# A 1 KB read of b ahead of the first loads, in a two-layer matmul kernel on one core

## The chip, the cores and the metric

The kernel runs on one core of a Trainium2 chip. The metric is the device time in microseconds (us) of one execution. The time before is 117.33 us, the median of 3 runs (117.23 to 117.46).

The engines are named as in the profile: PE is TensorE (PEld its weight loads), DVE is VectorE, ACT is ScalarE, POOL is GpSimd, SP is SyncE, which here does nothing but issue transfers.

## What is computed

```python
h = np.matmul(a, b)            # a: 1024 x 1024, b: 1024 x 2048, float32
h = 0.5 * h * (1 + np.tanh(np.sqrt(2 / np.pi) * (h + 0.044715 * h ** 3)))
return np.matmul(h, c).astype(np.float32)      # c: 2048 x 1024
```

## The kernel before

**Tiling.** M = K = P = 1024 and N = 2048, in tiles of 128 rows. The first product is made transposed: its result, after the gelu, is `hT`, with N on the partitions, in two halves of 512 columns of M. TensorE therefore needs a transposed (`aT`, by transposes through TensorE, line 145, copied out of PSUM by VectorE, line 146) and b as it lies in memory (`b1`, `b2`). The first 512 columns of N are computed plainly (`mm1`, line 114). The rest of the first product, and the whole second product, use a scheme with seven block products in place of eight (class `Seven`, products on line 212), with sums and differences of blocks on VectorE (line 170).

**Order.** The schedule is written out by hand: each engine does its instructions in the order of the program. Waits between engines are on semaphores that the framework sets. Transfers issued by SyncE and ScalarE share eight completion counters, given out in turn in the order of the program; GpSimd's transfers have eight others.

**Loads.** SyncE issues five loads at the start (lines 75 to 79), in float32, in this order:

- line 75: the first quarter of a for M's first half (`sta[:, 0, 0]`, 512 KB, 1 KB pieces),
- line 76: b's rows 0 to 255, first 512 columns (`stb[:, 0:2]`, 512 KB, 2 KB pieces; for each partition the rows p and p + 128),
- line 77: the same quarter of a's columns for M's second half (512 KB),
- line 78: the second quarter for the first half (512 KB),
- line 79: b's rows 256 to 383 (256 KB).

VectorE and ScalarE cast what these bring to bf16 (lines 110 and 108). GpSimd waits for the first of them by a copy of one column (`gate`, line 81), and then issues everything else as loads that cast on the way: the rest of a (`abq`, line 86), the rest of b (lines 89, 92, 98, 101) and all of c (line 104). Until the first data come, TensorE multiplies zeros (`stir`, line 125).

The order of the work at the start, on TensorE: five `stir`s; the transposes of the first quarter; matmuls for k = 0 and part of k = 1, once b's first rows are cast; the transposes of line 77's quarter (the group of eight at 8.47 us); and so on through the quarters, the last of which is `abq`'s fourth for M's second half.

**Stores.** The results leave in `done2` (line 431), called for each 128 x 512 block of the output, each by one transfer from SyncE (line 429), except that the second block to leave, `(i, l, j) == (0, 0, 1)`, is stored as two transfers of 256 columns. Three more stores of part of a block come at the very end (line 376), one of them from ScalarE. The transfers issued by SyncE and ScalarE are 24 in all: 5 loads, 16 in `done2`, 3 at the end.

A tile of 128 x 16 float32 called `room` is set aside among the constants and not used (line 55).

Of the kernel before, what the change touches and what calls it, by code (L numbers as in the profile page):

```python
# [9 lines left out]
F32 = mybir.dt.float32  # L10
# [9 lines left out]
def kernel(ctx, tc, a, b, c, out):  # L20
    nc = tc.nc
# [3 lines left out]
    H = 512  # L25
# [8 lines left out]
    consts = ctx.enter_context(tc.tile_pool(name="consts", bufs=1))  # L34
# [11 lines left out]
    def pieces(tag, bufs, shape, dt, name):  # L46
        return small.tile(shape, dt, name=name, tag=tag, bufs=bufs)
# [4 lines left out]
    gate = consts.tile([128, 1], F32, name="gate")  # L52
    g = consts.tile([128, 1], F32, name="g")

    consts.tile([128, 16], F32, name="room")

    c_sb = keep.tile([128, NT, P], BF16, name="c_sb")
    hT = [keep.tile([128, NT, H], BF16, name=f"hT{h}") for h in range(2)]
# [10 lines left out]
    def a_part(h, q):  # L69
        return av[:, 4 * h:4 * h + 4, ds(q * 256, 256)]  # L70

    def b_part(q):
        return bv[:, 2 * q:2 * q + 2, 0:H]

    nc.sync.dma_start(out=sta[:, 0, 0], in_=a_part(0, 0))
    nc.sync.dma_start(out=stb[:, 0:2], in_=b_part(0))
    nc.sync.dma_start(out=sta[:, 1, 0], in_=a_part(1, 0))
# [21 lines left out]
    for n in range(2):  # L99
        for k in range(0, KT, 4):  # L100
            nc.gpsimd.dma_start(out=b2[:, k:k + 4, ts(n, H)],
                                in_=bv[:, k:k + 4, ds(1024 + n * H, H)])
# [325 lines left out]
    def store(mt, q0, w, ot, eng=None):  # L428
        (eng or nc.sync).dma_start(out=out[ts(mt, 128), ds(q0, w)], in_=ot)

    def done2(i, l, j, p):
        if (i, l) == (1, 0):
            ot = pieces("o", 4, [128, H], F32, "ot")
            nc.vector.tensor_copy(ot, p)
            p = ot
        n = 2 if (i, l, j) == (0, 0, 1) else 1
        for q in range(n):
            r = ds(q * (H // n), H // n)
            store(4 * i + j, l * H + q * (H // n), H // n, p[:, r])

    def between2(n):
        if n == "P1":
# [11 lines left out]
        elif n == "P73":  # L454
            two.t4(two.t[1], 4)

    seven(two, done2, between2)


# [28 lines left out]
```

## Time and profile before

| What | Value |
|---|---|
| Median of 3 runs | 117.33 us (117.23 to 117.46) |
| The profiled execution, its own time | 117.6 us |
| Its span, from the first to the last instruction | 115.8 us |
| Granted TensorE clock | 1.00 |
| PE busy | 110.7 us (96%) |
| PEld busy | 77.1 us (67%) |
| DVE busy | 90.1 us (78%) |
| ACT busy | 51.4 us (44%) |
| POOL busy | 17.3 us (15%) |
| Chain that ended last | PE 79%, DMA 13%, POOL 5% |
| SyncE's queue (q1) | 4592 packets, 6.42 MB |
| GpSimd's queue (q0) | 8672 packets, 9.31 MB |

All times within the execution are counted from the start of the span. In a row of the timeline, the first number is the start, the second the time from the first start to the last end of the merged instructions, then the engine, the line, the operation, what it writes and reads, and how many there are; in brackets, the idle time of that engine just before, and what ended it. In the chain of waits, each row is a stretch of time that lay on the path to the last instruction: start, length, and what it was spent on. In the table by stretches, a row has the stretch, its length, each engine's busy time, then the granted clock, the DMA engines' share and the GB/s moved.

### The profile page before, as it was taken

The page shows a single profiled execution, that of the slowest core. Times are in us where ns is not written, and L with a number is a line of the kernel's source. Part 1 is how long each engine was busy: PE and PEld are TensorE (multiplying, and loading weights), DVE is VectorE, ACT ScalarE, POOL GpSimd, SP SyncE. Part 2 cuts the span into 40 slices and gives each one's busy share as a digit, 9 for nine tenths or more (in the row PEclk, how much of TensorE's full clock was granted, in tenths as well). Part 3 has the DMA queues.
Part 4 walks back from the last instruction along what each step waited for, and adds up shares of the span by engine and source line. Part 5 has one row for each costly group of instructions (what it writes and reads, how often), then busy time and mean ns, then how long its engine had stood idle before and what let it go on. Part 6 is the DMA issues. An engine that isn't in the chain of part 4 may idle for free.

```text
span 115.8 us, 1473 instructions
## 1 busy us (share of the span) xinstructions
PE 110.7 (96%) x544; PEld 77.1 (67%) x550; DVE 90.1 (78%) x108; ACT 51.4 (44%) x86; POOL 17.3 (15%) x29
## 2 busy tenths in 40 slices
PE   7889999999999999999999999999999999999990
PEld 6545555445777447888886444588888888888870
DVE  0247747689999998944789999999999986964581
ACT  5053000799268998066699339700043992000000
POOL 2497754222332000000000000000000000000000
PEclk9999999999999999999999999999999999999999
DMA  3999999999999999998000000070000002004994
GB/s 74 296 381 221 200 199 204 204 207 207 205 210 210 211 212 212 212 210 163 9 0 0 6 0 0 0 272 0 0 0 0 0 0 94 2 27 173 364 358 166
DMA packets 13414, 15.94 MB, mean 138 GB/s; under 512 B 736, under 2 KB 9184, under 8 KB 13408
## 3 DMA queue, kind: packets, MB, share of 16 engines
q0 software_dynamic: 8672, 9.31, 47.6%
q1 hardware_dynamic: 4592, 6.42, 15.7%
q10 hardware_dynamic: 144, 0.13, 0.3%
q8 instruction: 4, 0.07, 0.2%
q14 instruction: 2, 0.02, 0.0%
HBM read 20.97 MB, written 4.19 MB: 217 GB/s over the span
## 4 chain that ended last, share of the span: by engine, by line
PE 79%; DMA 13%; POOL 5%; issue 0%; DVE 0%
PE ps L212 76%; DMA abq<-in_a_dram 10%; DMA sta<-in_a_dram 3%; POOL abq L86 3%; PE ps L114 2%; POOL b L89 1%; POOL gate L81 1%; PE pt L145 1%; POOL b L92 0%; DVE ot L375 0%
## 5 line engine op out<-in xcount | busy, mean ns | idle before, releaser
L212 PE MATMUL ps<-x,s 128*128 128x512 f32 x128 | 29.6, 391 | 0.0
L212 PEld LDWEIGHTS ps<-x,s 128*128 128x128 f32 x128 | 24.0, 188 | 5.1
L212 PE MATMUL ps<-x,x 128*128 128x512 f32 x96 | 22.9, 394 | 0.0
L212 PEld LDWEIGHTS ps<-x,x 128*128 128x128 f32 x96 | 18.0, 188 | 3.9
L114 PE MATMUL ps<-aT,b 128*128 128x512 bf16 x62 | 15.7, 379 | 0.3 <-DVE b L110 0.2
L298 ACT ACTIVATE v<-ps 128x512 f32<-128x512 f32 x10 | 6.0, 598 | 19.1 <-PE ps L212 19.1
L212 PE MATMUL ps<-c_sb,hT 128*128 128x512 bf16 (+2 forms) x78 | 14.1, 336 | 0.1
L212 PE MATMUL ps<-x 128*128 128x512 f32 x56 | 13.2, 393 | 0.0
L212 PEld LDWEIGHTS ps<-x 128*128 128x128 f32 x56 | 10.2, 188 | 2.7 <-ACT u L298 0.4
L212 PEld LDWEIGHTS <-hT 128*128 128x128 bf16 x80 | 7.1, 98 | 7.0 <-issue 0.5
L118 ACT ACTIVATE hT<-ps 128x512 bf16<-128x512 f32 x14 | 7.3, 596 | 9.6 <-PE ps L114 9.6
L118 ACT ACTIVATE hT<-ot 128x512 bf16<-128x512 f32 x18 | 10.4, 623 | 2.1 <-DVE ot L303 2.0
L146 DVE COPY aT<-pt 128x512 bf16<-128x512 bf16 x16 | 6.7, 422 | 5.5 <-PE pt L145 5.4
L212 PE MATMUL ps<-aT,b 128*128 128x512 bf16 x46 | 10.6, 379 | 0.1
L303 DVE TENSOR_TENSOR ot<-ps,u 128x512 f32<-128x512 f32 x10 | 6.7, 688 | 5.2 <-ACT u L298 5.2
L303 DVE TENSOR_TENSOR ot<-ps,v 128x512 f32<-128x512 f32 x10 | 6.7, 688 | 4.9 <-DMA out_dram<-ot 3.9
L170 DVE TENSOR_TENSOR x<-c_sb 128x1024 fp32r<-128x1024 bf16 x8 | 9.2, 1216 | 0.0
L114 PEld LDWEIGHTS <-b 128*128 128x128 bf16 x64 | 5.7, 97 | 4.5 <-DVE b L110 0.3
L212 PEld LDWEIGHTS <-b 128*128 128x128 bf16 x48 | 4.6, 97 | 5.7 <-issue 0.3
L104 POOL DMA_DIRECT2D c_sb<-in_c_dram x8 | 5.6, 703 | 13.4 <-DMA b<-in_b_dram 11.1
L170 DVE TENSOR_TENSOR x<-b 128x1024 fp32r<-128x1024 bf16 (+1 forms) x4 | 7.0, 1751 | 0.6 <-issue 0.6
L298 ACT ACTIVATE u<-ps 128x512 f32<-128x512 f32 x10 | 5.9, 597 | 3.4 <-PE ps L212 3.2
(44 smaller groups left out, 110.7 us busy)
## 6 DMA issues: line engine op xcount, KB each, us to landing
c_sb<-in_c_dram POOLq DMA_DIRECT2D x8, 512.0 KB, 19.7
out_dram<-ot SPq DMA_DIRECT2D x14, 256.0 KB, 2.1
b<-in_b_dram POOLq DMA_DIRECT2D x6, 512.0 KB, 15.6
sta<-in_a_dram SPq DMA_DIRECT2D x3, 512.0 KB, 6.2
abq<-in_a_dram POOLq DMA_DIRECT2D x5, 256.0 KB, 8.0
stb<-in_b_dram SPq DMA_DIRECT2D x1, 512.0 KB, 5.4
b<-in_b_dram POOLq DMA_DIRECT2D x2, 256.0 KB, 8.3
stb<-in_b_dram SPq DMA_DIRECT2D x1, 256.0 KB, 7.2
```

The lines of the kernel that those rows point to most:

```text
L81: nc.gpsimd.tensor_copy(gate, sta[:, 0, 0, 3, 0:1])
L86: nc.gpsimd.dma_start(out=abq[:, q, h], in_=a_part(h, q))
L89: nc.gpsimd.dma_start(out=b1[:, 2 * q:2 * q + 2, 0:H], in_=b_part(q))
L104: nc.gpsimd.dma_start(out=c_sb[:, t:t + 2], in_=cv[:, t:t + 2])
L114: nc.tensor.matmul(p, b1[:, k, ts(t, 128)], aT[:, h, k], start=(k == 0), stop=(k == KT - 1))
L118: nc.scalar.activation(hT[h][:, t], p, AF.Gelu_apprx_tanh)
L145: nc.tensor.transpose(pt[:, n, ts(m, 128)], ab[:, m, ts(n, 128)], ident)
L146: nc.vector.tensor_copy(aT[:, h, 2 * q + n], pt[:, n])
L170: nc.vector.tensor_tensor(out=dst[:, r], in0=x[:, r], in1=y[:, r], op=op)
L212: nc.tensor.matmul(p[:, ds(c0, w)], l[:, k, ts(j, 128)], r[:, k, ds(c0, w)], start=(start and k == 0), stop=(k == self.kt - 1), skip_group ...
L298: nc.scalar.activation(st, p, AF.Copy)
L303: nc.vector.tensor_tensor(out=ot, in0=p, in1=st, op=ADD)
```

## The change

One transfer is put ahead of SyncE's five loads. It reads 16 float32 (64 bytes) from each of b's rows 0, 16, 32, ..., 240 into the first 16 partitions of `room`, which nothing reads. And the block that was stored by two transfers is stored by one, so that SyncE's and ScalarE's transfers are 24 as before.

```diff
-    consts.tile([128, 16], F32, name="room")
+    room = consts.tile([128, 16], F32, name="room")
...
+    nc.sync.dma_start(out=room[0:16], in_=b.rearrange("(x y) n -> x y n", y=16)[0:16, 0, 0:16])
     nc.sync.dma_start(out=sta[:, 0, 0], in_=a_part(0, 0))
     nc.sync.dma_start(out=stb[:, 0:2], in_=b_part(0))
     nc.sync.dma_start(out=sta[:, 1, 0], in_=a_part(1, 0))
...
             nc.vector.tensor_copy(ot, p)
             p = ot
-        n = 2 if (i, l, j) == (0, 0, 1) else 1
-        for q in range(n):
-            r = ds(q * (H // n), H // n)
-            store(4 * i + j, l * H + q * (H // n), H // n, p[:, r])
+        store(4 * i + j, l * H, H, p)
```

## Prediction

> **What bounds the kernel now.** I read the chain of waits first, then the timeline of the first 25 us, then the stretches' table of the loads. The chain says where an edit can count at all:
>
> ```profile
> 0.74 3.70 DMA sta<-in_a_dram
> 4.49 0.70 POOL gate L81
> ...
> 10.15 11.43 DMA abq<-in_a_dram
> 21.58 0.05 issue
> 21.63 0.40 PE pt L145 x4
> ...
> 27.73 11.44 PE ps L212 x49
> ...
> 39.21 23.73 PE ps L212 x105
> ...
> 73.79 39.11 PE ps L212 x188
> ...
> 112.93 0.29 DVE ot L375
> ```
>
> From 21.63 on it is TensorE alone to the end: 91 us in which it hardly waits. So a microsecond won or lost in TensorE's start is won or lost at the end, and nothing between 22 us and the last stores is worth anything unless TensorE is made to wait. Before 21.6 it is loads. The timeline shows which landing TensorE's early work hangs on:
>
> ```profile
> 4.46 0.69 DVE L110 CAST ab<-sta 128x1024 bf16<-128x1024 f32 x1 [4.46 <-DMA sta<-in_a_dram]
> 6.62 0.36 DVE L110 CAST b<-stb 128x128 bf16<-128x128 f32 x2 [0.55 <-DMA stb<-in_b_dram]
> 6.90 1.47 PE L114 MATMUL ps<-aT,b 128*128 128x512 bf16 x6 [0.17 <-DVE b L110]
> 7.99 0.43 DVE L110 CAST ab<-sta 128x512 bf16<-128x512 f32 x1 [0.68 <-DMA sta<-in_a_dram]
> 8.47 0.62 PE L145 MATMUL pt<-ident,ab 128*128 128x128 bf16 x8
> 21.62 0.23 PEld L145 LDWEIGHTS <-abq 128*128 128x128 bf16 x4 [0.64 <-DMA abq<-in_a_dram]
> ```
>
> Each of SyncE's loads is used at once when it lands: 4.44 (first quarter of a), 6.59 (b's first 256 rows), 7.97 (the next quarter of a). From 8.47 TensorE runs with gaps of a tenth at most, except one of about 0.3 us ahead of 21.63, where the last cast load of a lands. That load cannot come sooner than the stream ahead of it. So the whole front hangs on the stream of loads, and it moves as one: SyncE's 2.36 MB first, GpSimd's cast loads behind them.
>
> **How fast that stream runs.** SyncE has issued everything by 3.53 us, long before the data are in:
>
> ```profile
> 0.74 0.42 SPq L75 DMA_DIRECT2D sta<-in_a_dram  x1
> 1.22 0.50 SPq L76 DMA_DIRECT2D stb<-in_b_dram  x1
> 1.77 0.46 SPq L77 DMA_DIRECT2D sta<-in_a_dram  x1
> 2.27 0.51 SPq L78 DMA_DIRECT2D sta<-in_a_dram  x1
> ```
>
> ```profile
> 1.80:2.50 0.70, 0.70 (x3) 0.61 (x2) 0.00 (x0) 0.43 (x2) 0.00 (x0) 1.00 0.75 110
> 2.50:4.00 1.50, 1.50 (x5) 1.15 (x5) 0.00 (x0) 0.00 (x0) 0.00 (x0) 1.00 1.07 350
> 4.00:5.50 1.50, 1.07 (x9) 0.65 (x7) 0.69 (x1) 0.00 (x0) 1.01 (x2) 1.00 0.93 253
> 5.50:8.50 3.00, 2.49 (x17) 1.29 (x16) 1.55 (x5) 1.45 (x3) 3.00 (x5) 1.00 1.07 373
> ```
>
> The last number of a row is GB/s. There are two slow places. One is the start, 110 GB/s: the first packets of a. The other is 4.0 to 5.5 us, 253 GB/s, which is when b's first 256 rows are read. The landings say the same: the 512 KB of b take 6.59 - 4.44 = 2.15 us, the two loads of 512 KB of a behind them 7.97 - 6.59 = 1.38 and 9.37 - 7.97 = 1.40. So 2.15 - 1.38 = **0.77 us** are lost on b's first rows. Rows 256 to 383 of b, loaded last, do not show it: 256 KB from 9.37 to 10.07, 0.70 us, half of 1.40. The packet records agree: a 2 KB packet takes 84 ns, but between 4.0 and 6.1 us some sixty of b's 256 take 130 to 500 ns; among the last 128 none does.
>
> **The change, part by part.**
>
> 1. *One more issue at the head of SyncE's queue.* SyncE's five loads follow each other at 0.48, 0.55, 0.50 and 0.55 us; the smallest transfers on this queue (the last stores, 64 KB in 128 rows) still take 0.33 to 0.39 us to issue, and some 0.05 lies between. For sixteen rows I take the low end, 0.33 + 0.05 = **0.38 us**. The trace has no issue of sixteen rows, so the bounds are 0 (all of the issue time goes with the number of rows) and 0.55 (a full load's step); 0.38 is the nearest row. All five loads move back by it, and nothing hides it: the first quarter of a is waited for by VectorE and GpSimd from 0 to 4.46 us.
>
> 2. *1 KB more to move.* Sixteen packets against 2,000 on this queue: nothing by size. If each of sixteen engines takes one, its wait lies in the 0.38 us in which the next load is not there yet.
>
> 3. *b's first rows are touched before they are needed.* The touched rows, 0, 16, ..., 240, span just the 2 MB that the 512 KB load reads. What it saves isn't shown by any row: between 0 and the whole 0.77. Less than nothing has a ground too small to price, 1 KB being added. I take the whole 0.77: b's rows 256 to 383 have the same pitch and packet size and no loss, so the loss goes with being first in b, and a's slow 0.7 us at the start is of the same kind; both are over once a tensor has been read from. That is nearer to "first use" than to "how it is laid out".
>
> 4. *The start of a.* At 110 instead of 350 GB/s, 0.70 us lose 0.70 x (350 - 110)/350 = 0.48 us. If that slowness belongs to the first use of the queue rather than of a, the touch takes it upon itself: between 0 and 0.48 saved. I take 0: the touch reads b, not a.
>
> 5. *The store that is not split* (at 75.1 and 75.5 us, SyncE). One issue of 0.46 us goes, in a stretch where SyncE next waits for VectorE (the store at 76.06) and then has nothing until 95 us. The chain there is TensorE. Nothing, and from the third block on the stores stand in the same places of the same eight completion counters, since one more load and one store less cancel.
>
> 6. *No new wait.* Nobody reads the touched tile. What waits behind the new issue are SyncE's five loads (counted in 1) and, through line 81's copy, GpSimd's cast loads: their issue from 5.14 on moves by up to 0.38. Their first packets appear at 8.8 us, as SyncE's run dry, so I count the drain as their limit, not the issue.
>
> **Sum.** The first quarter of a lands at 4.44 + 0.38 = 4.82; b at 6.59 + 0.38 - 0.77 = 6.20; the next quarter of a at 7.97 - 0.39 = 7.58. VectorE, in order: cast to 5.53, copy of the first transposes 6.03 to 6.45, then b's cast at 6.45 instead of 6.62. So the first matmuls win only 0.17, but they have 0.27 to spare ahead of 8.47, and the transposes there start near 8.1. From there on all landings and TensorE stand **0.39 us earlier**, the last cast load included. The profiled execution took 117.6 us (span 115.8, and 1.8 around it), so it would be 117.2; the median of the runs is 117.33, from which I take the same 0.39: **116.94**.
>
> A rule of the Trainium skill speaks against item 3. "DMA: Bandwidth & Descriptors", section "Latency and other measured facts", reports copies at half rate when rows lie a large power of two apart, whatever was read before, and infers that they meet in one memory channel. The load of b's first rows alternates between rows 1 MB apart, and the last 256 KB of b do not, so the slow stretch would be the pattern's by that rule. The touch would save nothing and the sum would be +0.38. Against it stands a: its quarters alternate between rows 512 KB apart, at 373 GB/s.
>
> **Rivals.**
>
> - *Nothing is bought* (0.26): b's slowness is its access pattern's, or something else at 4 to 6 us, or the touch reaches too few engines. Then only item 1 is left: 117.33 + 0.38 to 0.55 = 117.71 to 117.88. Slow packets go on until 6.1, well past the first packet of each engine, which speaks for it.
> - *Half is bought* (0.18): a first use costs a, by item 4, 0.48; if b's costs as much and the rest is pattern, the saving is eaten by the issue: 117.33 + 0.38 - 0.48 = 117.23, within 0.2%.
> - *The start is spared too* (0.06): 0.39 + 0.48 earlier, 116.46.
> - *The cast loads become late* (0.08, slower): GpSimd's issue hangs on the first quarter of a, which lands 0.38 later. If their descriptors are what 8.8 us waits for, and not the drain, their stream moves to 9.2, a hole opens behind SyncE's, and the landing at 21.58, for which TensorE waits already, comes 0.38 later: 117.71. It decides as soon as the first cast packets come later than SyncE's last. Against it: 3.7 us between issue and first packet, and no pause of the engines at 8.8.
>
> My forecast, 0.39 earlier (0.42), has its own range of 116.7 to 117.1, by the issue's size.
>
> **How the numbers follow.** About 0.2%, 0.23 us, is what a measurement here can tell from no change. Faster: 0.42 + 0.06 = 0.48. Same: 0.18. Slower: 0.26 + 0.08 = 0.34. The range runs from 116.5 (the start spared) to 117.85 (a full issue, nothing bought).
>
> **What would show it.** Item 1: the first sta issue at about 1.1, VectorE's first cast at about 4.85. Item 3: from that landing to b's cast 1.4 to 1.6 us and not 2.15, and a rate near 350 GB/s in that stretch. The sum: transposes of the third group near 8.1 instead of 8.47, the last cast load at about 21.2. Wrong: a first cast at 4.85 with b's landing at 7.0; a first cast at 4.46 (the issue costs nothing, or the start is spared); cast packets that begin after 9 us with engines idle before; any new wait after 25 us.

## The result and the profile after

The changed kernel took 117.70 us, the kernel before 117.27 us (medians of 14 runs each), and the ratio of the times is **1.0041** (95% interval 1.0027 to 1.0055): 0.48 us slower by the ratio, 0.43 by the medians. One of the changed kernel's 14 runs, 119.32 us at a granted clock of 0.983, is left out of the ratio. I had forecast 0.39 us faster. The time lies inside the range that I gave, on the wrong side, next to that of the rival "nothing is bought" (117.71 to 117.88).

Line numbers of the changed kernel are one higher from line 76 on. Its timeline at the start (start, length, engine, line, operation, tiles; in brackets the idle time before and what ended it):

```profile
0.74 0.39 SPq L75 DMA_DIRECT2D room<-in_b_dram  x1
1.19 0.41 SPq L76 DMA_DIRECT2D sta<-in_a_dram  x1
...
5.14 0.69 DVE L111 CAST ab<-sta 128x1024 bf16<-128x1024 f32 x1 [5.14 <-DMA sta<-in_a_dram]
...
7.02 0.36 DVE L111 CAST b<-stb 128x128 bf16<-128x128 f32 x2 [0.26 <-DMA stb<-in_b_dram]
...
8.38 0.55 DVE L111 CAST ab<-sta 128x512 bf16<-128x512 f32 x1 [0.66 <-DMA sta<-in_a_dram]
...
8.99 0.62 PE L146 MATMUL pt<-ident,ab 128*128 128x128 bf16 x8 [0.17 <-DVE ab L111]
```

The touch takes 0.39 us to issue and 0.06 to hand over, so every load behind it is issued **0.45 us** later (1.19 against 0.74). The casts that wait for the loads move by 0.68, 0.40 and 0.39 us: VectorE's first cast from 4.46 to 5.14, b's cast from 6.62 to 7.02, that of line 77's quarter (line 78 here) from 7.99 to 8.38. One profile's landings scatter by some 0.35 us (see the first experiment), so these agree with 0.45. Nothing clear of that scatter is won back: the trace tells a load's landing in sixteen steps, and by the middle one b's first rows come 2.06 us behind the first quarter of a, against 2.03 before. The table by stretches, each moved by 0.45 us against the one of before, so that the same loads stand in the same rows (last number GB/s):

```profile
2.25:2.95 0.70, 0.70 (x3) 0.61 (x2) 0.00 (x0) 0.00 (x0) 0.00 (x0) 1.00 0.70 120
2.95:4.45 1.50, 1.50 (x5) 1.15 (x5) 0.00 (x0) 0.00 (x0) 0.00 (x0) 1.00 1.07 332
4.45:5.95 1.50, 0.99 (x4) 0.28 (x3) 0.69 (x1) 0.00 (x0) 0.78 (x2) 1.00 0.88 276
5.95:8.95 3.00, 2.63 (x18) 1.50 (x18) 1.67 (x5) 1.51 (x3) 3.00 (x5) 1.00 1.04 365
```

110, 350, 253, 373 before; 120, 332, 276, 365 now. Both slow places are still there: the start, and the stretch in which b's first 256 rows are read, although sixteen of those rows had been touched and had landed by 2.2 us. The chain of waits of the changed kernel:

```profile
2.19 6.17 DMA sta<-in_a_dram
8.36 0.02 issue
8.38 0.56 DVE ab L111
8.94 0.05 issue
8.99 0.62 PE pt L146 x8
...
25.18 87.99 PE ps L213 x408
```

It now leads from line 78's load (line 77's in the kernel before) by one cast to TensorE, which does not wait again. The wait of 0.3 us ahead of 21.63 is gone: in the kernel before's profiled execution the last cast load of a landed late, at 21.58, here at 20.49. It was one straggler: fifteen of that load's sixteen steps had come by 19.92. That is why the spans differ by only 0.2 us (115.8 and 116.0) where the third group of transposes differs by 0.52 (8.47 and 8.99). These are one execution each; the medians differ by 0.43.

### The profile page after: what moved, and what is told of

It is laid out like the page before. It is cut to its first block, busy times and chain, and to the rows that moved or that the text cites. A ratio compares the mean times of both kernels' runs of the same rounds, so it can differ in the third digit from the quotient of the medians.

```text
span 116.0 us, 1479 instructions
## 1 busy us (share of the span) xinstructions
PE 111.5 (96%) x550; PEld 77.4 (67%) x550; DVE 90.0 (78%) x108; ACT 51.4 (44%) x86; POOL 17.3 (15%) x29
## 3 DMA queue, kind: packets, MB, share of 16 engines
q1 hardware_dynamic: 4480, 6.43, 15.5%
## 4 chain that ended last, share of the span: by engine, by line
PE 90%; DMA 5%; SPq 1%; DVE 1%; issue 0%
PE ps L213 76%; PE ps L115 11%; DMA sta<-in_a_dram 5%; PE pt L146 3%; DVE ab L111 0%; SPq L77 0%; SPq L76 0%; SPq L75 0%; DVE ot L376 0%
## 5 line engine op out<-in xcount | busy, mean ns | idle before, releaser
L115 PE MATMUL ps<-aT,b 128*128 128x512 bf16 x64 | 16.1, 379 | 0.0
L213 PE MATMUL ps<-aT,b 128*128 128x512 bf16 x48 | 10.7, 379 | 0.0
```

Of the source, the lines that this page charges most:

```text
L115: nc.tensor.matmul(p, b1[:, k, ts(t, 128)], aT[:, h, k], start=(k == 0), stop=(k == KT - 1))
L213: nc.tensor.matmul(p[:, ds(c0, w)], l[:, k, ts(j, 128)], r[:, k, ds(c0, w)], start=(start and k == 0), stop=(k == self.kt - 1), skip_group ...
```

## The experiments

"Before" in the ratios is the kernel before, run on the same chip in the same session. Its own time was 117.20 to 117.26 us. Theory N, formed from the profile after: the touch buys nothing and costs its issue at the head of SyncE's queue.

**The store alone** (e1_store_one): the kernel before with

```diff
-        n = 2 if (i, l, j) == (0, 0, 1) else 1
-        for q in range(n):
...
+        store(4 * i + j, l * H, H, p)
```

> The kernel before with only the store edit: the second block leaves in one transfer, 23 transfers in all. Theory N (the whole loss is the extra issue at the head of SyncE's queue): ratio to before 1.000, within 0.15%, every landing before 22 us where it was. Rival S (the loss is, at least in part, the store's): ratio 1.001 to 1.004.

Ratio 0.9996 (0.9974 to 1.0017). The store is worth nothing that could be measured, as item 5 had it. The landings did not stay where they were: in this profile the first cast came at 4.12 instead of 4.46 and line 77's quarter was cast at 8.34 instead of 7.99, though the loads are those of the kernel before. So a landing read from one profile is good to some 0.35 us; the issue times, and the ratios over several runs, are firmer.

**The touch from another queue** (e2_touch_on_act):

```diff
-    nc.sync.dma_start(out=room[0:16], in_=b.rearrange("(x y) n -> x y n", y=16)[0:16, 0, 0:16])
+    nc.scalar.dma_start(out=room[0:16], in_=b.rearrange("(x y) n -> x y n", y=16)[0:16, 0, 0:16])
```

> The changed kernel with the same 1 KB read issued by ScalarE at 0.74 us, so that SyncE's loads keep their place. Theory N (the touch buys nothing, only its issue costs): ratio to before 1.000, first cast at 4.46, b's cast at 6.6, transposes of the third group at 8.45. Theory F (the touch spares b a first use, and the issue ate it): b's cast 0.2 to 0.7 us sooner, at 5.9 to 6.4, ratio 0.994 to 0.998. Rival X (the sixteen small packets themselves disturb the loads): first cast later than 4.6, ratio above 1.001.

Ratio 1.0009 (0.9987 to 1.0032). The timeline:

```profile
0.74 0.45 ACTq L75 DMA_DIRECT2D room<-in_b_dram  x1
...
6.59 0.36 DVE L111 CAST b<-stb 128x128 bf16<-128x128 f32 x2
...
7.94 0.54 DVE L111 CAST ab<-sta 128x512 bf16<-128x512 f32 x1 [0.52 <-DMA sta<-in_a_dram]
```

b's cast at 6.59 (6.62 before) and line 77's quarter at 7.94 (7.99): the touch saves nothing, even when it delays nothing. Only the first cast is later, 4.70; one engine's share of that load landed late, the middle one of its sixteen steps at 4.07 as before (4.13).

**The touch behind the loads** (e8_touch_last): the same line, moved below line 79's load.

> The changed kernel with the same 1 KB read issued behind SyncE's five loads instead of ahead of them. Theory N (the price is the place at the head of the queue): ratio to before 1.000, within 0.15%, loads issued and landing as in the kernel before. Rival (the read itself disturbs the stream, or the transfers' counters do): ratio 1.002 or more.

Ratio 1.0007 (0.9987 to 1.0028); b's cast at 6.56, line 77's quarter at 7.95. With the same packets and the same 24 transfers, the loss of 0.41% is gone: the price is the place at the head of the queue.

**Two touches** (e14_two_touches): the touch's line twice, the second into `room[32:48]`.

> The changed kernel with the 1 KB read issued twice at the head of SyncE's queue. Theory N (the loss is the issues'): SyncE's first large load issued at 1.64, first cast at 5.1 to 5.6, ratio to before 1.007 to 1.009, twice the loss. Rival (the loss is a single event of the first transfer): ratio 1.003 to 1.005, as with one.

SyncE's first large load was issued at 1.64 and cast at 5.16; b's cast came at 7.53, line 77's quarter at 8.91, each about 0.5 us later than with one touch, so the issue adds up as theory N has it. But the ratio is 1.0155 (1.0100 to 1.0210), about twice what I expected. The table by stretches shows the rest (the number before the last two is the granted clock):

```profile
5.04:8.46 3.42, 1.88 (x15) 1.23 (x15) 2.02 (x5) 0.93 (x2) 3.27 (x5) 1.00 0.98 312
8.46:11.87 3.41, 3.41 (x16) 1.76 (x14) 1.67 (x4) 1.76 (x5) 3.21 (x5) 0.50 1.25 291
```

In the first of these stretches TensorE, waiting for the later loads, was busy 1.88 of 3.42 us; in the next it was granted half its clock. But this is the profile of a run of 120.20 us, one of two in six with a granted clock of 0.98; the other four, at 0.995 to 1.000, still took 118.52 to 119.43. So the clock explains a part of the excess, and the rest is open. More on the clock below.

**The touch of a** (e3_touch_a): the same, with a's rows 0, 32, ..., 480.

```diff
-    nc.sync.dma_start(out=room[0:16], in_=b.rearrange("(x y) n -> x y n", y=16)[0:16, 0, 0:16])
+    nc.sync.dma_start(out=room[0:16], in_=a.rearrange("(x y) n -> x y n", y=32)[0:16, 0, 0:16])
```

> The changed kernel with the 1 KB read from a's rows 0, 32, ..., 480 in place of b's. If the slow start of the first load is the first use of a, it goes: the first cast comes at about 4.6 to 4.75 instead of 5.14, and the ratio to before is 1.000 or below. If the start is slow whatever was touched (theory N), it is as in the changed kernel: first cast at 4.9 to 5.15, ratio 1.003 to 1.005.

Ratio 1.0038 (1.0010 to 1.0066), first cast at 4.81, b's cast at 7.08, line 77's quarter at 8.44. The first cast lies between the two expectations and is 0.33 sooner than with b touched; the later landings, which set the time, are as with b touched. The same issue, the same loss.

What, then, makes b's first load slow? Four runs moved it about.

**b's load in two** (e4_split_b):

```diff
-    nc.sync.dma_start(out=stb[:, 0:2], in_=b_part(0))
+    nc.sync.dma_start(out=stb[:, 0], in_=bv[:, 0, 0:H])
+    nc.sync.dma_start(out=stb[:, 1], in_=bv[:, 1, 0:H])
```

(and the store not split).

> The kernel before with line 76 split in two loads, b's rows 0 to 127 and then 128 to 255, so that no load alternates between rows 1 MB apart; one store is not split, so 24 transfers. Theory P (b's slow stretch is the alternation's): 253 GB/s in 4.0 to 5.5 us becomes 340 or more, the next quarter of a (line 77's) is cast at 7.2 to 7.5 us instead of 7.99, ratio 0.994 to 0.997. Theory F (first use of b): the first of the two is the slow one and the quarter of a stays near 7.99, ratio about 1.000, k = 0 starting earlier.

Ratio 1.0077 (1.0045 to 1.0110); 200 GB/s in 4.0 to 5.5 us. The first 256 KB landed 1.69 us after the quarter of a (4.74 to 6.43), the second 0.66 us later, at full speed; line 77's quarter was cast at 8.54. The time is longer than by either expectation. So it is not the alternation between rows 1 MB apart.

**a before b** (e5_a_second): lines 76 and 77 exchanged.

> The kernel before with lines 76 and 77 in the other order: both halves of a's first quarter, then b's first rows. Theory T (whatever is read at 4 to 6 us is slow, b or not): 4.0 to 5.5 us stays under 300 GB/s with a in it, and b behind it comes at full speed, 1.4 us after the quarter of a. Theory F (b's first large read is slow wherever it stands): a at 340 GB/s or more up to 5.8 us, then b takes 1.8 to 2.2 us. In time: the first matmuls begin some 1.3 us later by either, and the third group of transposes no longer waits for its load, ratio 1.000 to 1.010.

Ratio 1.0287 (1.0243 to 1.0331). In the table by stretches, a is read in the first row and b in the second:

```profile
4.00:5.50 1.50, 1.50 (x8) 1.00 (x6) 0.69 (x1) 0.00 (x0) 1.29 (x2) 1.00 1.02 347
5.50:7.00 1.50, 1.15 (x11) 0.83 (x9) 0.42 (x1) 0.00 (x0) 1.50 (x4) 1.00 0.82 200
```

The slowness moves with b; theory T (that time of the execution is slow) falls. The time is far worse than by either expectation: TensorE then waits 2.45 us for b and gets half its clock from 8.99 to 12.40 us.

**b ahead of a** (e6_b_first): line 76 above line 75.

> The kernel before with line 76 ahead of line 75: b's first rows are the first load of all. Theory F: both slow stretches stay, each with its tensor's first large read: b lands near 4.6 and a's quarter takes 1.7 us or more behind it. Theory T: start slow, and 4.0 to 5.5 us under 300 GB/s with a in it. If the slowness at 4 to 6 us belongs to 2 KB pieces behind 1 KB pieces, it goes, and a's quarter takes 1.4 us. Ratio 1.000 to 1.010, since the first transposes now wait for the second load.

Ratio 1.0283 (1.0267 to 1.0300). b is slow as the very first load too (120 GB/s in 1.8 to 2.5 us, 233 in 2.5 to 4.0, 308 in 4.0 to 5.5, landing at 5.34), and a's quarter behind it takes 1.53 us: a's own "first use" costs little when something else was first. Theory F had 1.7 or more there.

**b's first rows twice** (e7_b_twice): before line 76, the same 512 KB into a spare tile.

> The kernel before with b's first rows loaded twice, first into a spare tile that nothing reads, then as line 76 does: 512 KB more. Theory F: the first copy takes 1.9 to 2.2 us and the second 1.4. Pattern theory P: both take 1.9 to 2.2. Theory T: slow until about 6 us, then 1.4 a load. The rest moves later by 1.4 us (F, T) or 2.1 us (P).

121.14 us (one time). The first copy took 1.93 us (4.11 to 6.04), the second, of the same bytes, 2.99 (to 9.03), with 285 GB/s in 5.5 to 7.0 us. One late step makes up 1.03 us of that; by the middle of their sixteen steps the copies took 1.54 and 2.07. Reading the very same rows just before spares nothing. Theory F falls, with a touch as large as the load itself.

**The layout** (three kernels, line 76's source alone changed; the destination and the 2 KB pieces stay). The pitch is the distance in memory from the start of one piece to that of the next; as each of b's rows is 8 KB long, line 76 reads 2 KB pieces at a pitch of 8 KB.

```diff
-    nc.sync.dma_start(out=stb[:, 0:2], in_=b_part(0))
+    # e9_b_contiguous: rows 0 to 63 whole
+    nc.sync.dma_start(out=stb[:, 0:2], in_=b[0:64].rearrange("(k r) (s n) -> (r s) k n", k=2, n=H))
+    # e10_b_other_rows: rows 512 to 767
+    nc.sync.dma_start(out=stb[:, 0:2], in_=bv[:, 4:6, 0:H])
+    # e11_a_at_b_pitch: a, as if its rows were 8 KB
+    nc.sync.dma_start(out=stb[:, 0:2], in_=a.rearrange("(r t) k -> r (t k)", t=2)
+                      .rearrange("(x p) n -> p x n", p=128)[:, 0:2, 0:H])
```

> The kernel before, but line 76 reads b's rows 0 to 63 whole, 512 KB in one piece of memory, still in 2 KB pieces; so the part of the first product that needs b's first 256 rows is computed from other values. Theory L (the slow stretch comes of 2 KB pieces at 8 KB pitch, read by all queues at once): it goes, 340 GB/s or more in 4.0 to 5.5 us, and the load takes 1.4 us. If anything first read from b is slow: 1.9 to 2.2 us as before.

> The kernel before, but line 76 reads b's rows 512 to 767 at the same pitch; the part of the first product that needs b's first 256 rows is computed from other values. Theory L: slow as before, under 300 GB/s in 4.0 to 5.5 us, 1.9 to 2.2 us for the load. If it is the place in memory of b's first 2 MB that is slow: 1.4 us.

> The kernel before, but line 76 reads 512 KB of a in b's way: 2 KB pieces 8 KB apart, 1 MB between the two of a partition; b's first 256 rows are so replaced by values of a. Theory L: slow, under 300 GB/s in 4.0 to 5.5 us, 1.9 to 2.2 us for the load. If it is b and not the pitch: 1.4 us.

The stretch 4.0 to 5.5 us of each, first b in one piece:

```profile
4.00:5.50 1.50, 1.50 (x10) 1.01 (x9) 0.73 (x2) 0.00 (x0) 1.19 (x2) 1.00 0.94 333
```

other rows of b at the same pitch:

```profile
4.00:5.50 1.50, 1.50 (x8) 0.96 (x7) 0.69 (x1) 0.00 (x0) 1.12 (x2) 1.00 0.92 243
```

and a at b's pitch:

```profile
4.00:5.50 1.50, 1.50 (x8) 0.89 (x6) 0.69 (x1) 0.00 (x0) 1.03 (x2) 1.00 0.96 248
```

333, 243 and 248 GB/s; the load itself took 1.25, 2.19 and 2.13 us. It is neither b nor its first rows: **in line 76's place, 2 KB pieces 8 KB apart are slow, from a just as from b, and the same amount of b in one piece is not.** (In the last of the three, a had been read from for two microseconds, and the real first use of b, line 79's load, took 0.73 us: full speed.) The load in one piece also covers 0.5 MB of memory instead of 2; but line 77's load is spread over 2 MB that nothing had read before it (a's rows 512 to 1023, pieces 4 KB apart), and took 1.38 us in the kernel before.

**But who pays?** In e9 the loads behind line 76's became slower: line 77's quarter of a took 1.85 us instead of 1.38, and line 79's load, which keeps the pitch, 1.13 instead of 0.70. So I timed that kernel, and one in which both of SyncE's loads of b come in one piece:

```diff
-    nc.sync.dma_start(out=stb[:, 2], in_=bv[:, 2, 0:H])
+    nc.sync.dma_start(out=stb[:, 2], in_=b[64:96].rearrange("r (s n) -> (r s) n", n=H))
```

> The same kernel as in e9_b_contiguous (line 76 reads 512 KB of b in one piece, so part of the first product is computed from other values), now timed. If what the loads win reaches the end: line 77's quarter 0.5 us or more sooner, ratio 0.994 to 0.997. If the loss only moves to line 79's load, the first that is left with 8 KB pitch, and the cast loads behind it start no sooner: ratio 0.998 to 1.002.

> The kernel before with lines 76 and 79 both reading b in one piece each (512 KB and 256 KB, 2 KB pieces), so part of the first product is computed from other values. No load from SyncE has 8 KB pitch left. If the pitch is what costs, SyncE's loads end 0.6 to 0.8 us sooner (line 79's landing at 9.3 to 9.5 instead of 10.07) and the cast loads start sooner by as much. If that reaches the end: ratio 0.993 to 0.997. If TensorE is held by something else: 0.998 to 1.001.

With line 76 alone: ratio 1.0026 (0.9995 to 1.0057). Its profile is of a run of 118.20 us, among the longer ones (117.23 to 118.50): fifteen of the load's sixteen steps had come by 5.29 us and the last at 6.39, and line 77's quarter landed at 8.62, later than in the kernel before. With both: ratio 1.0080 (1.0056 to 1.0104), worse than by either expectation. There SyncE's two loads of b were fast and line 79's landed at 9.76 instead of 10.07, though line 77's quarter took 1.96 us; but now GpSimd's load of line 92, the first left with that pitch, is slow. Its stretch, and the same one of the kernel before:

```profile
11.00:12.00 1.00, 1.00 (x10) 0.52 (x7) 0.88 (x2) 0.00 (x0) 0.52 (x1) 1.00 1.08 115
```

```profile
11.00:12.00 1.00, 0.95 (x8) 0.55 (x8) 0.65 (x2) 0.00 (x0) 0.37 (x1) 1.00 1.37 194
```

115 GB/s where the kernel before moves 194; it lands at 12.86 instead of 11.98, and TensorE waits 0.73 us for it at 12.90. So what line 76's load saves is lost again behind it, on either queue: in part by the next load at that pitch, in part by line 77's, whose pitch is 4 KB. One might take this for a price that the first load at 8 KB pitch pays once for all, since lines 79 and 92 run at full speed in the kernel before. The runs do not bear that out. In e7 the second copy was slow behind the first; and in e6 and e12, where lines 76 and 79 had both read at that pitch, line 92's load landed 1.73 and 2.76 us behind the one ahead of it, against 0.64 in the kernel before. (GpSimd issued its loads later in those two, from 7.57 and 7.21 us on instead of 5.14.)

**A touch at the load's own pitch** (e16_touch_all_rows): every one of b's first 256 rows, 32 bytes of each, from ScalarE.

```diff
+    nc.scalar.dma_start(out=room.rearrange("p (k n) -> p k n", k=2), in_=bv[:, 0:2, 0:8])
```

> The changed kernel with the touch issued by ScalarE at 0.74 us and made of 32 bytes from each of b's rows 0 to 255, the load's own pitch, in place of sixteen rows. If the first read at 8 KB pitch pays once and a small one can pay: line 76's load takes 1.4 us instead of 2.15, line 77's quarter lands at 7.3 to 7.6, ratio 0.994 to 0.998. If only a load of full size pays: landings as in the kernel before, ratio 0.999 to 1.002. If the 256 small packets hold up a's first load: first cast at 4.7 or later, ratio 1.002 or more.

Ratio 1.0004 (0.9982 to 1.0026); b's cast at 6.57, line 77's quarter at 7.99, 261 GB/s in 4.0 to 5.5 us. The 256 small packets had landed by 4.26 and changed nothing. A small read does not pay for a large one.

**b's load beside a's** (e12_b_on_act): line 76's load issued by ScalarE.

```diff
-    nc.sync.dma_start(out=stb[:, 0:2], in_=b_part(0))
+    nc.scalar.dma_start(out=stb[:, 0:2], in_=b_part(0))
```

> The kernel before with line 76's load issued by ScalarE at 0.74 us, beside SyncE's loads instead of between them. If the slow stretch costs by keeping all queues at b's rows together (theory L), mixing them with a's hides it: the first quarter of a lands at 4.7 to 5.1, b at 4.9 to 5.6 instead of 6.59, line 77's quarter at 6.3 to 7.2 instead of 7.97, ratio 0.993 to 0.998. If the slowness is only spread over both: that quarter at 7.7 to 8.0, ratio 0.999 to 1.003.

Ratio 1.0253 (1.0209 to 1.0298), far outside both expectations: b landed at 6.24, a's first quarter only at 6.52, line 77's at 7.87. Sooner by a tenth for the quarter that matters; but TensorE stood idle from 5.1 to 7.29 us, and the clock was 0.50 from 8.03 to 11.44. No version that I tried beats the kernel before.

## Why the prediction was wrong

- *What bounds the kernel* held in the main. SyncE's landings set the start, TensorE the rest, and the loss at the loads reached the end: 0.45 us of issue, 0.48 by the ratio. One reading was wrong: I took the landing at 21.58, for which TensorE waits, for the end of the stream of loads, and forecast it at about 21.2. It was one late step of that execution, and the same load landed at 20.49 in the changed kernel although its whole stream was later.
- *Item 1* was right in kind and low in size: 0.38 forecast, 0.45 measured. An issue of sixteen rows takes 0.39 us, that of 512 pieces of a 0.41 to 0.51; the time hardly goes with the number of pieces, and the gap to the next is 0.06.
- *Item 2* held: the touch's packets by themselves cost nothing that could be measured (e2, e8).
- *Item 3 is the step that failed*: "I take the whole 0.77 ... the loss goes with being first in b". It measured nothing: 6.59 against 6.62 us for b's cast when the touch costs nothing (e2), and no more with all 256 rows touched (e16) or read whole (e7). Other rows of b, or a in b's place, at the same pitch took 2.19 and 2.13 us, and b in one piece 1.25 (e9, e10, e11): the loss goes with the layout of the load in that place, not with b's first use. The observation that I leaned on was true, rows 256 to 383 have the same pitch and no loss; but line 79's load differs from line 76's in two things, that b had been read and that it comes behind all the other loads, and I credited only the first. e11 separates them: there line 79's is the first read of b, and it is fast.
- *The rule that spoke against it.* The Trainium skill's rule in "DMA: Bandwidth & Descriptors", section "Latency and other measured facts", that copies slow down with rows a large power of two apart, was right in kind: the layout decides here too. But I read it too widely. It has 207 GB/s at 512 KiB and 164 at 2 MiB, and half of the full 214 only at 4 and 8 MiB; no run here has the rows of neighbouring partitions so far apart, and 8 KB lies far below. So none shows whether its loss and this one have one cause. The alternation over 1 MB, which I took for the rule's case, is not it (e4). And a's quarters at 373 GB/s were no argument against a pitch, since within each group a's pieces are 4 KB apart, not 8.
- *Item 4*: nothing clear of the scatter was saved at the start, as taken (110 against 120 GB/s).
- *Item 5* held (e1). *Item 6* held in that no wait came up: the first cast packets came at 9.28 us instead of 8.82, though GpSimd's issue moved by 0.68 us and not 0.38. That they wait for SyncE's drain isn't shown: in e7 they began at 9.20 us, while SyncE's last load, line 81's there, had its first step at 11.19.
- *The sum's last step*, that 0.39 less at the loads would be 0.39 less at the end, was never put to the test by the change. e15 suggests that it would not have come through in full: SyncE's loads ended 0.3 us sooner there, and the time was 0.8% longer, with TensorE waiting 0.73 us for line 92's load.
- *Open*: why a load in such pieces is slow at the front of the stream, and which of the later ones pays when it is not. "Only the first load at that pitch" fits the kernel before, e10 and e11, and not e6, e7 and e12; no run here tests a reason.

## What to carry to other kernels

A transfer ahead of the first load costs its whole issue, 0.45 us here for 1 KB, if the first load is what everything waits for; behind the loads, or on an idle queue, the same transfer cost nothing that could be measured. Before touching memory to warm it, read the suspect twice (e7) or read something else in the same way: one look at the same pieces from another tensor (e11), or at the same tensor in another layout (e9), tells "first use" from "layout". And where two loads differ in one thing that you see, look for the second thing, their order among all loads, before you credit the first.

## What the runs showed of the hardware

- *The layout of a load at the front of the stream sets its speed.* 512 KB in 2 KB pieces 8 KB apart took 2.13 to 2.19 us, whichever tensor they came from (the kernel before, e10, e11), against 1.25 in one piece (e9) and about 1.4 in 1 KB pieces 4 KB apart. Later loads of 256 KB at 8 KB pitch took 0.64 to 0.73 us there, full speed. But what is saved in one piece is lost again by the loads behind (e9, e13, e15), so no time was won.
- *TensorE lost half its clock for 3.41 us after a stretch in which it was idle much of the time, even in short pauses.* In five profiles the granted clock was 0.50 for 3.41 us. In the 3.41 us just before, TensorE had been busy 1.07 (e5), 0.92 (e6), 1.21 (e7), 1.14 (e12) and 1.88 us (e14); the longest single pause was 2.2 to 2.9 us in the first four and 0.67 us in e14. The length of a pause alone doesn't decide: pauses of 0.97 and 0.95 us (e4, e13) cost no clock, and e3 kept its clock with 2.21 us busy from 4.23 to 7.64. What the half clock costs shows in e5, where three runs at 0.982 to 0.986 took 120.90 to 121.08 us and one at 1.000 took 119.56: some 1.4 us. Even without it the last is 2.3 us above the kernel before. The Trainium skill's "TensorE: Matmul & The Clock Gate", section "Part 1: The HAM clock gate", has the clock halve after an idle window of about 3.4 us; here less idle time was enough, 1.88 us busy of 3.42 in e14.
